# A hybrid attention and SwiGLU layer on one core: every SBUF tile that TensorE reads moved to a multiple of 512 bytes

## The chip, the core and the metric

The kernel runs on one core of a Trainium2 chip. The metric is device time in microseconds (us): three runs of the kernel before gave 1419.07, 1419.39 and 1425.46, median 1419.39. Besides these there is one profiled execution, from which all rows below come.

An SBUF address here is a number of bytes inside a partition. For every tile only its *residue* matters in what follows: its start address modulo 512.

## The reference, cut to what matters

One layer over 256 latent tokens `x` and 256 context tokens `ctx`, all float32, width 2048:

```python
mod = silu_c @ w_ada + b_ada                        # six rows of 2048: shift, scale, gate, twice
h   = rms_norm(x,   g_attn) * (1 + sc_a)  + sh_a
hc  = rms_norm(ctx, g_attn) * (1 + csc_a) + csh_a
q, k, v of four head groups = h @ w_in, hc @ w_in   # neighbourhood, GQA, latent (MLA), differential
x = x + gt_a * (concat(attention outputs) @ w_out)
h = rms_norm(x, g_ffn) * (1 + sc_f) + sh_f
x = x + gt_f * ((silu(h @ ffn_wg) * (h @ ffn_wu)) @ ffn_wd)   # inner width 5632
return rms_norm(x, g_final)
```

The large products with `w_in`, `w_out`, `ffn_wg`, `ffn_wu` and `ffn_wd` are nearly all of the work.

## The kernel before

**Products in three parts.** Each float32 operand is split into a high part of type float32r and a low part (the rest, again float32r). `split` (line 119) makes `whi` from a loaded weight tile `raw` with a copy on ScalarE (ACT, line 127) and `wlo` with a subtraction on VectorE (DVE, line 130). The activations have such pairs too: `h` (hi and lo) for the first layer norm, `o_hi`/`o_lo` for the attention outputs (line 878), `h2_hi`/`h2_lo` for the second norm (line 911), `ah`/`al` for the SwiGLU product (line 1024). `mm3s` (line 145) then issues three matmuls per product, at lines 150, 151 and 153. In most of them the *stationary* operand (loaded into the array, 128 x 128) is a slice of the activations of 128 tokens, and the *moving* operand is a row of 512 weight columns. In the names of the profile the moving operand stands first: `acc<-whi,h_hi` streams `whi` past `h_hi`. Each matmul has its own weight load on PEld, which reads the stationary operand of the next matmul while the present one still streams.

**The order of the work.** The main stream goes through the weights in tiles of 256 x 512 (`stream_w`, one DMA of 512 KB on SyncE's queue each, four `raw` buffers, six `whi` and six `wlo`). From one such tile come 12 matmuls of 512 columns for two token tiles. Side tasks (softmax, transposes, the adaLN columns of `w_ada`) are traced in between by `side.pump`, by times written in the program.

**The stages.** To about 300 us: adaLN, the norm, and the columns of NA and GQA with moving `whi`/`wlo` and stationary `h`. To about 560 us: the other columns and the attention heads. Then the output projection (stationary `o_hi`, `o_lo`); its last third and the first block of SwiGLU keep their weight tiles in the pool `rt` (`keep_w`, line 920: the first tile of each of the two comes from the stream pool, the other seven from `rt`). Then SwiGLU: blocks of gate and up (`gu`, line 986, stationary `h2`) and of down (line 1047, stationary `ah`, `al`). The last 512 columns are done one token tile after the other: the first four weight tiles of token tile 0 are held in a pool `rt2` (line 1067), the others in the stream pool.

**Where tiles lie.** Pools are stacks: those of the left side grow from `const` upwards, those of `side="right"` from the top of SBUF downwards. A tile's address is the sum of the sizes below it, in steps of 32 bytes. So an odd-sized small tile shifts all that lies behind it on its side: `ss2` (line 872) shifts what comes behind it in `res`, `ss3` (line 1010) what comes behind it in `ff`:

```python
small = ctx.enter_context(tc.tile_pool(name="small", bufs=6))     # line 82
ss2 = res.tile([P, 2, 4], F32, name="ss2")                        # line 872
ss3 = ff.tile([P, 2, 5], F32, name="ss3")                         # line 1010
```

Of the kernel before, what the change touches and what calls it, by code (L numbers as in the profile page):

```python
# [10 lines left out]
F32 = mybir.dt.float32  # L11
# [6 lines left out]
P = 128  # L18
# [13 lines left out]
class Side:  # L32
    """Instructions traced in between the weight tiles of the main stream.

    A task is a generator that yields (time it takes of the tensor engine, time its
    results need) in us; its next stage is traced once the main stream has gone on
    for that long. Lanes are worked on independently, `width` tasks of a lane at once.
    """

# [48 lines left out]
def hybrid_dit_kernel(ctx: ExitStack, tc: tile.TileContext, a, out):  # L88
    nc = tc.nc
    pe, act, dve, pool, sp = nc.tensor, nc.scalar, nc.vector, nc.gpsimd, nc.sync  # L90
    side = Side()

    const = ctx.enter_context(tc.tile_pool(name="const", bufs=1))
    small = ctx.enter_context(tc.tile_pool(name="small", bufs=6))
    stream = ctx.enter_context(tc.tile_pool(name="stream", bufs=3))
    dram = ctx.enter_context(tc.tile_pool(name="dram", bufs=1, space=bass.MemoryType.DRAM))
    psA = ctx.enter_context(tc.tile_pool(name="psA", bufs=4, space=PSUM))
    psM = ctx.enter_context(tc.tile_pool(name="psM", bufs=4, space=PSUM))

    po, p_h, p_kv, p_s0 = ExitStack(), ExitStack(), ExitStack(), ExitStack()  # L100
# [4 lines left out]

    # ------------------------------------------------------------ helpers
    def misc():
# [13 lines left out]
    def split(raw, n, keep=None):  # L121
        """hi and lo parts of raw [128, k, n], one pair per k"""
        out_ = []
        pool_, bufs = keep or (stream, WB)
        for k in range(raw.shape[1]):
            hi = pool_.tile([P, n], F32R, name="whi", tag="whi", bufs=bufs)
            act.copy(hi, raw[:, k])  # L127
            newest["act"] = nc.cur_bb.bb.instructions[-1]
            lo = pool_.tile([P, n], F32R, name="wlo", tag="wlo", bufs=bufs)
            dve.tensor_tensor(out=lo, in0=raw[:, k], in1=hi.bitcast(F32), op=ALU.subtract)  # L130
            newest["dve"] = nc.cur_bb.bb.instructions[-1]
            out_.append((hi, lo))
        return out_
# [5 lines left out]
    def after(*ins):  # L139
        """what the block traces on an engine of ins is issued behind them"""  # L140
        st = ExitStack()
        for i in ins:
            st.enter_context(tc.issue_after(i))
        return st

    def mm3s(jobs, w_left=False):
        """l @ r from their parts for each (bank, l, r, start, stop); the products with the
        low part of the weights come after all the others"""
        for dst, l, r, start, stop in jobs:
            pe.matmul(dst, lhsT=l[0], rhs=r[0], start=start, stop=False)  # L150
            pe.matmul(dst, lhsT=l[0 if w_left else 1], rhs=r[1 if w_left else 0], start=False, stop=False)  # L151
        for dst, l, r, start, stop in jobs:
            pe.matmul(dst, lhsT=l[1 if w_left else 0], rhs=r[0 if w_left else 1], start=False, stop=stop)  # L153
# [13 lines left out]

    # ------------------------------------------------------------ tokens and small vectors
    x_t = {}
# [14 lines left out]

    ident = const.tile([P, P], F32, name="ident")
    make_identity(nc, ident)
# [26 lines left out]

    # ------------------------------------------------------------ normalised tokens, features on partitions
    xnT = [None] * 8
# [34 lines left out]
    def ada_pe(pr):  # L250
        """shift and scale of chunks 2 pr, 2 pr + 1 for both streams: column tile j of the
        tensor engine takes chunk j % 2 of the shift (j < 2) or the scale"""
        mv = misc()
        for k2 in range(0, KC, 2):
            raw = sb0.tile([P, 2, 2, 256], F32, name="araw", tag="araw", bufs=4)
            for kk in range(2):
                sp.dma_start(raw[:, kk], ada_two[:, k2 + kk, :, pr * 256:(pr + 1) * 256])
            for kk in range(2):
                kc = k2 + kk
                for j in range(4):  # L260
                    pe.matmul(mv[32 * j:32 * j + 32, :P], lhsT=cs32[:, kc, :], rhs=raw[:, kk, j // 2, tsl(j % 2)], start=(kc == 0), stop=(kc == KC - 1), skip_group_check=True)  # L261
            yield 0.5, 1.3
        mvs = sb0.tile([P, P], F32, name="mvs", bufs=2)
        act.copy(mvs, mv[:, :P])
        yield 0.0, 0.5
        cp = misc()
        pe.transpose(cp[:, :P], mvs, ident)
        cpv = cp[:, :P].rearrange("p (s j t) -> p s j t", s=2, j=2)[:, :, :, 0:2]
        k2 = slice(2 * pr, 2 * pr + 2)

        def col(c):
            return c.unsqueeze(2).to_broadcast([P, 2, 2])

        dve.tensor_tensor(out=scg[:, k2, :], in0=cpv[:, 1], in1=col(colA1[:, 16 + 2 * pr:18 + 2 * pr]), op=ALU.add)
        dve.tensor_tensor(out=scg[:, k2, :], in0=scg[:, k2, :], in1=col(colB[:, k2]), op=ALU.mult)
        dve.tensor_tensor(out=sha[:, k2, :], in0=cpv[:, 0], in1=col(colA[:, k2]), op=ALU.add)
        yield 0.1, 0.0
# [35 lines left out]

    # ------------------------------------------------------------ NA and GQA columns: summed over groups of K chunks on SBUF
    na_qT = kv.tile([P, 4, S], F32, name="qT", bufs=3)
# [5 lines left out]

    # ---- second use of w_ada: gate and FFN columns
    mcol = {s: const.tile([P, KC], F32, name=f"mcol{s}") for s in (2, 3, 4, 5)}
# [31 lines left out]
    parts = [[0], [1], [2, 3], [4, 5], [6, 7]]  # L355
# [7 lines left out]
    def block(c0, prs, first, units):  # L363
        """one block of 512 columns over the K chunks of prs; a unit is (matmul operands, where its bank is added)"""
        accs = [acc() for _ in units]
        for pr in prs:
            w = stream_w(w_in, 2 * pr, c0, 512)
            for i, (form, where) in enumerate(units):
                mm3s([form(accs[i], w, 2 * pr + kk, pr == prs[0] and kk == 0, pr == prs[-1] and kk == 1) for kk in range(2)], c0 == NA_K)
                if pr == prs[-1]:  # L370
                    for dst, src in where(accs[i]):
                        add_up(dst, src, first)
                side.pump(1.3, 2.0)
# [31 lines left out]
    tabs, bias = {}, []  # L405
# [3 lines left out]
    def prepare():  # L409
        """rope tables with the GQA gains in them, the NA bias with its mask, lambda"""  # L410
        xa = sb0.tile([P, 2, 4, S], F32, name="xa", tag="x_t", bufs=2)
# [8 lines left out]
        mask = xb[:, 768:832]  # L420
# [76 lines left out]

    # ------------------------------------------------------------ the four head groups
    p_at = ExitStack()
# [22 lines left out]
    def proj(c0, n, toks, evac, hook=None):  # L522
        """columns c0.. of the input projection for token tiles toks; evac(t, psum) is a task"""
        accs = [acc() for _ in toks]
# [26 lines left out]
    def rope(dst, src, ct, st, nh, hd):  # L551
        """dst = src * ct + swap(src) * st over nh heads of width hd; ct, st [128, hd]"""
        half = hd // 2
# [9 lines left out]
    def soft(score, bias=None):  # L563
        """exp(score - max) of a [128, 512] score tile, and the reciprocal of its sum"""
        if bias is not None:
# [44 lines left out]
    def gate_rows(seg, pool_):  # L610
        """the gate of seg as one row on all partitions, by way of DRAM"""
        ps = misc()
# [17 lines left out]

    # ---- grouped-query attention
    def head_rstd(ps, nh):
# [53 lines left out]

    # ---- multi-head latent attention
    c64, s64 = table("rope_c64", 64), table("rope_s64", 64)
# [109 lines left out]

    # ---- differential attention
    def dk_evac(t, ps):  # L800
# [63 lines left out]

    # ------------------------------------------------------------ output projection and residual
    side.finish(*gate_tasks)
# [4 lines left out]
    gta = gate_rows(2, res)  # L871
    ss2 = res.tile([P, 2, 4], F32, name="ss2")
    p_o3, p_oh = ExitStack(), ExitStack()
# [89 lines left out]

    # ------------------------------------------------------------ SwiGLU
    def gu_jobs(ps, w_, k2, t):
# [43 lines left out]
    gate_f = add_ada(5, 4.0, stream_raw)  # L1009
    ss3 = ff.tile([P, 2, 5], F32, name="ss3")  # L1010
    gfin = ff.tile([P, D], F32, name="gfin")
# [45 lines left out]

    # ------------------------------------------------------------ the last columns one token tile after the other, final norm
    p_h2.close()
# [89 lines left out]
```

## Time and profile before

| | before |
|---|---|
| median of three runs | 1419.39 us |
| span of the profiled execution, first to last instruction | 1415.0 us |
| difference, what lies around the span | 4.4 us |
| PE (matmuls) busy | 1375.5 us, 97% |
| DVE busy | 914.9 us, 65% |
| ACT busy | 618.9 us, 44% |
| HBM traffic | 221 GB/s over the span |
| mean granted TensorE clock | 0.996 of full speed |

The duration that the profile gives for a matmul overlaps with the next one. What a matmul costs in a dense row of matmuls is the distance from its start to the next start; the rows of the timeline give the starts.

### The profile page before, as it was taken

How to read it: one execution, taken by the hardware profiler on the slowest of the kernel's cores; microseconds unless marked ns; L12 is line 12 of the kernel's file. 1: busy time of each engine (PE TensorE's matmuls, PEld its weight loads, DVE VectorE, ACT ScalarE, POOL GpSimd, SP SyncE). 2: the span in 40 equal slices, each digit the busy share in tenths (PEclk: the TensorE clock that was granted, in tenths of full speed). 3: DMA queues.
4: the chain of work that ended last, by engine and by line, in shares of the span. 5: the costliest groups of instructions: out<-in, count | busy, mean ns of one | idle time of the engine just before them, and what ended most of it. 6: DMA issues, size and time to landing. Idle time of an engine off the chain costs nothing.

```text
span 1415.0 us, 19888 instructions
## 1 busy us (share of the span) xinstructions
PE 1375.5 (97%) x7082; PEld 1082.3 (76%) x7082; DVE 914.9 (65%) x1623; ACT 618.9 (44%) x1180; POOL 34.1 (2%) x46
## 2 busy tenths in 40 slices
PE   6999999998999999999999999999999999999997
PEld 4766778766876687777877788888888888888886
DVE  3565679988888728779677854445545565555465
ACT  3522223464333525557444454444444443444443
POOL 1020000100000000000000000000000000000000
PEclk9999999999999999999999999999999999999999
DMA  9998896668879726356888876666666556666653
GB/s 324 322 318 278 282 312 215 205 215 264 270 246 298 230 90 235 124 175 188 290 272 281 293 239 194 185 190 180 191 182 183 182 182 196 183 188 181 185 167 139
DMA packets 183607, 313.78 MB, mean 222 GB/s; under 512 B 14002, under 2 KB 53972, under 8 KB 182356
## 3 DMA queue, kind: packets, MB, share of 16 engines
q1 hardware_dynamic: 179104, 302.03, 66.9%
q0 software_dynamic: 1056, 7.36, 1.3%
q10 hardware_dynamic: 3348, 3.13, 0.7%
q8 instruction: 55, 0.90, 0.3%
q14 instruction: 44, 0.36, 0.1%
HBM read 310.36 MB, written 2.11 MB: 221 GB/s over the span
## 4 chain that ended last, share of the span: by engine, by line
PE 74%; DMA 12%; DVE 8%; ACT 2%; issue 2%; POOL 0%; SPq 0%; ACTq 0%; POOLq 0%; DVEq 0%
PE acc L150 23%; PE acc L151 22%; PE acc L153 22%; DMA raw<-in_w_ada_dram 7%; DVE ada_acc L337 3%; DMA raw<-in_w_in_dram 3%; PE m L261 3%; DVE wlo L130 2%; DMA raw<-in_ffn_wg_dram 1%; ACT whi L127 1%; PE m L830 1%; DMA raw<-in_ffn_wu_dram 1%; DMA rowsB<-in_rows_dram 1%; PE m L232 1%; PE m L541 1%
## 5 line engine op out<-in xcount | busy, mean ns | idle before, releaser
L130 DVE TENSOR_TENSOR wlo<-raw,whi 128x512 fp32r<-128x512 f32 (+1 forms) x764 | 491.2, 682 | 354.0 <-ACT whi L127 345.8
L127 ACT CAST whi<-raw 128x512 fp32r<-128x512 f32 (+1 forms) x764 | 433.0, 614 | 618.6 <-PE acc L151 414.1
L150 PE MATMUL acc<-whi,h_hi 128*128 128x512 f32 x704 | 280.7, 399 | 2.5 <-ACT whi L127 2.5
L151 PE MATMUL acc<-whi,h_lo 128*128 128x512 f32 x704 | 279.1, 396 | 0.0
L153 PE MATMUL acc<-wlo,h_hi 128*128 128x512 f32 x704 | 195.7, 397 | 0.2 <-DVE wlo L130 0.2
L337 DVE SCALAR_TENSOR_TENSOR ada_acc<-raw,cs,ada_acc 128x512 f32<-128x512 f32 x210 | 157.1, 748 | 38.0 <-DMA raw<-in_w_ada_dram 28.7
L150 PE MATMUL acc<-whi,h 128*128 128x512 f32 (+1 forms) x416 | 166.8, 403 | 5.3 <-ACT whi L127 3.4
L150 PEld LDWEIGHTS acc<-whi,h_hi 128*128 128x128 f32 x704 | 132.6, 188 | 36.3 <-ACT whi L127 5.1
L151 PE MATMUL acc<-whi,h 128*128 128x512 f32 (+1 forms) x416 | 157.8, 381 | 0.0
L153 PEld LDWEIGHTS acc<-wlo,h_hi 128*128 128x128 f32 x704 | 132.6, 188 | 32.8 <-DVE wlo L130 0.7
L151 PEld LDWEIGHTS acc<-whi,h_lo 128*128 128x128 f32 x704 | 132.6, 188 | 31.4
L150 PE MATMUL acc<-whi,ah 128*128 128x512 f32 (+1 forms) x364 | 141.3, 390 | 0.0
L151 PE MATMUL acc<-whi,al 128*128 128x512 f32 (+1 forms) x364 | 140.9, 389 | 0.0
L153 PE MATMUL acc<-wlo,h 128*128 128x512 f32 (+1 forms) x416 | 114.4, 379 | 0.2 <-DVE wlo L130 0.2
L150 PEld LDWEIGHTS acc<-whi,h 128*128 128x128 f32 x416 | 78.3, 188 | 30.5 <-issue 11.0
L153 PE MATMUL acc<-wlo,ah 128*128 128x512 f32 (+1 forms) x364 | 98.7, 389 | 0.0
L153 PEld LDWEIGHTS acc<-wlo,h 128*128 128x128 f32 x416 | 76.0, 188 | 15.7 <-DVE wlo L130 1.4
L151 PEld LDWEIGHTS acc<-whi,h 128*128 128x128 f32 x416 | 78.4, 188 | 12.5 <-issue 1.2
L150 PEld LDWEIGHTS acc<-whi,ah 128*128 128x128 f32 x364 | 68.6, 188 | 15.5
L151 PEld LDWEIGHTS acc<-whi,al 128*128 128x128 f32 x364 | 68.6, 188 | 15.4
L153 PEld LDWEIGHTS acc<-wlo,ah 128*128 128x128 f32 x364 | 67.7, 188 | 15.6
L150 PE MATMUL acc<-whi,o_hi 128*128 128x512 f32 x128 | 51.8, 406 | 0.0
(228 smaller groups left out, 1278.6 us busy)
## 6 DMA issues: line engine op xcount, KB each, us to landing
raw<-in_w_ada_dram SPq DMA_DIRECT2D x112, 512.0 KB, 4.6
raw<-in_ffn_wg_dram SPq DMA_DIRECT2D x88, 512.0 KB, 3.8
raw<-in_ffn_wu_dram SPq DMA_DIRECT2D x88, 512.0 KB, 3.9
raw<-in_ffn_wd_dram SPq DMA_DIRECT2D x88, 512.0 KB, 4.6
raw<-in_w_in_dram SPq DMA_DIRECT2D x72, 512.0 KB, 5.0
araw<-in_w_ada_dram SPq DMA_DIRECT2D x128, 256.0 KB, 4.8
raw<-in_w_out_dram SPq DMA_DIRECT2D x32, 512.0 KB, 3.9
araw<-in_w_ada_dram SPq DMA_DIRECT2D x16, 512.0 KB, 5.7
```

The source lines that it names most:

```text
L127: act.copy(hi, raw[:, k])
L130: dve.tensor_tensor(out=lo, in0=raw[:, k], in1=hi.bitcast(F32), op=ALU.subtract)
L150: pe.matmul(dst, lhsT=l[0], rhs=r[0], start=start, stop=False)
L151: pe.matmul(dst, lhsT=l[0 if w_left else 1], rhs=r[1 if w_left else 0], start=False, stop=False)
L153: pe.matmul(dst, lhsT=l[1 if w_left else 0], rhs=r[0 if w_left else 1], start=False, stop=stop)
L232: pe.transpose(ps[:, kk * S + t * P:kk * S + (t + 1) * P], x_t[2 * w + t][:, tsl(2 * pr + kk)], ident)
L261: pe.matmul(mv[32 * j:32 * j + 32, :P], lhsT=cs32[:, kc, :], rhs=raw[:, kk, j // 2, tsl(j % 2)], start=(kc == 0), stop=(kc == KC - 1), ski ...
L337: dve.scalar_tensor_tensor(out=acc_, in0=raw[:, kk, :], scalar=cs[:, 0, kc:kc + 1], in1=acc_, op0=ALU.mult, op1=ALU.add)
L541: pe.transpose(ps[:, tsl(j)], src[:, tsl(j)], ident)
L830: pe.matmul(sc, lhsT=df_qT[hb, h, tsl(t)], rhs=df_kT[h // 2][hb, h % 2, :], start=True, stop=True)
```

## The change

Two pads are added, one on each side, and three small tiles move. `ss2` and `ss3` go into `const`, `ident` into a pool of its own behind a pad of 32 bytes, and a pad of 480 bytes stands at the outer end of the right side.

```diff
     const = ctx.enter_context(tc.tile_pool(name="const", bufs=1))
+    ss2 = const.tile([P, 2, 4], F32, name="ss2")
+    ss3 = const.tile([P, 2, 8], F32, name="ss3")
     small = ctx.enter_context(tc.tile_pool(name="small", bufs=6))
+    pad = ctx.enter_context(tc.tile_pool(name="pad", bufs=1))
+    pad.tile([P, 8], F32, name="left_pad")
+    ident = pad.tile([P, P], F32, name="ident")
     stream = ctx.enter_context(tc.tile_pool(name="stream", bufs=3))
...
+    edge = ctx.enter_context(tc.tile_pool(name="edge", bufs=1, side="right"))
+    edge.tile([P, 120], F32, name="edge_pad")
...
-    ident = const.tile([P, P], F32, name="ident")
...
-    ss2 = res.tile([P, 2, 4], F32, name="ss2")
...
-    ss3 = ff.tile([P, 2, 5], F32, name="ss3")
```

The rest of the diff blanks comments. The built programs have the same instructions in the same order on all five engines. One wait differs: GpSimd's load of `gfin` (used from line 1045 on) no longer waits for four DMA queues, only for DVE, PE and ACT.

The residues (start address modulo 512) as the built programs have them:

| tiles | before | after |
|---|---|---|
| `raw`, `whi`, `wlo` of the stream pool; `h` | 384 | 0 |
| `o_hi`, `o_lo`; `whi`, `wlo` in `rt` | 416 | 0 |
| `h2_hi`, `h2_lo`; `ah`, `al`; `whi`, `wlo` in `rt2` | 480 | 0 |
| all of the right side (`cqT`, `ckvT`, `qT`, `kT`, `v`, `pT`, `p`, `tok`, `x_t`, `araw`, ...) | 480 | 0 |
| `ident` | 256 | 0 |

Slices that TensorE reads from these tiles start at multiples of 512 bytes behind the tile's start (128 float32 columns are 512 bytes), so a slice has its tile's residue. Only the slices of `cs32` (32 columns) do not.

## Rows read from the trace of the kernel before

**Rows 1.** The page, busy time of PE: us, share, instructions.

```profile
PE 1375.5 (97%) x7082; PEld 1082.3 (76%) x7082; DVE 914.9 (65%) x1623; ACT 618.9 (44%) x1180; POOL 34.1 (2%) x46
```

**Rows 2.** Windows: stretch, length, busy us per engine, PEclk, DMA share, GB/s.

```profile
680.00:765.00 85.00, 83.80 (x369) 66.91 (x368) 63.37 (x101) 35.10 (x62) 0.00 (x0) 1.00 0.82 277
1000.00:1100.00 100.00, 100.00 (x437) 80.61 (x436) 49.99 (x78) 44.05 (x78) 0.00 (x0) 1.00 0.62 184
```

**Rows 3.** The chain in order of time: start us, us, what.

```profile
676.67 5.56 DMA raw<-in_w_ada_dram
...
800.55 3.78 DMA raw<-in_ffn_wg_dram
...
1006.34 0.94 PE acc L153 x4
```

**Rows 4.** Timeline of PE near the end: start us, us, line, operands.

```profile
1379.71 1.10 PE L153 MATMUL acc<-wlo,ah 128*128 128x512 f32 x4
...
1388.14 1.10 PE L153 MATMUL acc<-wlo,ah 128*128 128x512 f32 x4
1389.08 0.39 PE L150 MATMUL acc<-whi,ah 128*128 128x512 f32 x1
...
1394.53 0.40 PE L150 MATMUL acc<-whi,ah 128*128 128x512 f32 x1
...
1395.93 0.39 PE L150 MATMUL acc<-whi,ah 128*128 128x512 f32 x1
```

**Rows 5.** Timeline of PE, weights kept in the pool rt.

```profile
635.42 0.39 PE L150 MATMUL acc<-whi,o_hi 128*128 128x512 f32 x1
...
638.14 0.39 PE L150 MATMUL acc<-whi,o_hi 128*128 128x512 f32 x1
...
647.09 0.39 PE L150 MATMUL acc<-whi,h_hi 128*128 128x512 f32 x1
...
649.89 0.39 PE L150 MATMUL acc<-whi,h_hi 128*128 128x512 f32 x1
```

**Rows 6.** Timeline of PE, output projection from the stream pool.

```profile
588.07 1.10 PE L153 MATMUL acc<-wlo,o_hi 128*128 128x512 f32 x4
...
590.87 1.10 PE L153 MATMUL acc<-wlo,o_hi 128*128 128x512 f32 x4
```

**Rows 7.** Timeline of PE, input projection, 512 columns.

```profile
511.72 1.07 PE L153 MATMUL acc<-wlo,h 128*128 128x512 f32 x4
...
514.44 1.07 PE L153 MATMUL acc<-wlo,h 128*128 128x512 f32 x4
```

**Rows 8.** Groups of PE, 800 to 1400 us, by form: count, busy us, mean ns.

```profile
L150 PE MATMUL acc<-whi,h_hi 128*128 128x512 f32 x498 | 198.1, 398 | 0.2 <-ACT whi L127 0.2
L151 PE MATMUL acc<-whi,h_lo 128*128 128x512 f32 x499 | 197.8, 396 | 0.0
L153 PE MATMUL acc<-wlo,h_hi 128*128 128x512 f32 x500 | 137.4, 396 | 0.0
L150 PE MATMUL acc<-whi,ah 128*128 128x512 f32 x340 | 135.0, 397 | 0.0
```

**Rows 9.** Groups of PE on the page, whole span.

```profile
L150 PE MATMUL acc<-whi,h_hi 128*128 128x512 f32 x704 | 280.7, 399 | 2.5 <-ACT whi L127 2.5
L150 PE MATMUL acc<-whi,o_hi 128*128 128x512 f32 x128 | 51.8, 406 | 0.0
```

**Rows 10.** Groups of DVE and ACT that make or use pairs, 800 to 1400 us.

```profile
L130 DVE TENSOR_TENSOR wlo<-raw,whi 128x512 fp32r<-128x512 f32 x425 | 273.8, 688 | 253.7 <-ACT whi L127 250.5 <-PE acc L153 3.0
L127 ACT CAST whi<-raw 128x512 fp32r<-128x512 f32 x424 | 242.0, 618 | 322.7 <-PE acc L151 305.8 <-DMA raw<-in_ffn_wg_dram 7.6 <-DMA raw<-in_ffn_wd_dram 3.3
L1042 DVE TENSOR_TENSOR x<-x,y 128x512 f32<-128x512 f32 x6 | 3.8, 682 | 0.0
```

**Rows 11.** Timeline of PE, input projection, 320 columns.

```profile
364.92 0.75 PE L153 MATMUL acc<-wlo,h 128*128 128x320 f32 x4
...
368.44 0.75 PE L153 MATMUL acc<-wlo,h 128*128 128x320 f32 x4
```

## The prediction

> **What bounds the kernel now.** I read the page's busy times first: PE is busy for 1375.5 of 1415.0 us [rows 1], so TensorE is the first suspect, but such a share does not say whether anything else sets its pace. The windows and the chain of waits do, stage by stage [rows 2, 3]. Between 680 and 765 us DMA has a share of 0.82 and 277 GB/s, PE is idle for 1.2 us, and the chain passes through DMA landings and DVE; its last such piece in the first half of SwiGLU is a landing that starts at 800.55 us. Behind it the chain is PE alone up to the last matmul. In the window from 1000 to 1100 us PE is busy for 100.00 of 100.00 us at the full granted clock (1.00), with DMA at 0.62, DVE at 49.99 us and ACT at 44.05 us. So for the last 600 us the time is the number of matmuls times the distance from one start to the next. The diff changes no instruction. Whether it changes the time hangs on one question: does that distance depend on where the operands lie?
>
> **The trace of before answers it by accident**, since its pools have three residues. I looked for places where the same code runs with other residues, and divided the time between starts by the matmuls between them.
>
> - Near the end, moving `whi`/`wlo` of the stream pool (384), stationary `ah`/`al` (480): from 1379.71 to 1388.14 us stand 36 matmuls of 512 columns, 8.43 / 36 = 0.2342 us each [rows 4].
> - The next 24 are the same loop with the weights held in `rt2`, which lies at 480 as `ah` does: 1389.08 to 1394.53 us, 5.45 / 24 = 0.2271 us. Then the stream pool again: six in 1.40 us, 0.2333 us [rows 4].
> - In `rt`, weights at 416 with `o_hi`/`o_lo` at 416: 12 in 2.72 us, 0.2267 us. A few us later the same pool with `h2` at 480: 12 in 2.80 us, 0.2333 us [rows 5].
> - Output projection, 384 against 416: 12 in 2.80 us, 0.2333 us [rows 6]. Input projection, `whi` and `h` both at 384: 12 in 2.72 us, 0.2267 us [rows 7].
>
> Equal residues (384, 416 or 480 alike) give 0.2267 us, unequal ones 0.2333 to 0.2342 us. So it is not the place of one operand but whether moving and stationary rows start at the same place in a frame of 512 bytes. That fits what happens at a time: PEld reads the next stationary slice while the matmul streams its row, and both read SBUF. It is not the region of SBUF either: `rt` is one pool and shows both values. After the change every pair is equal, at 0.
>
> [...]
>
> **The change part by part.** The durations are those of the profiled execution. Its span of 1415.0 us lies 4.4 us below the median of 1419.39 us; I take the gain from the median and leave the 4.4 us as they are.
>
> *Term A, 800 to 1400 us.* The groups count 498 + 499 + 500 matmuls with `h2` and three groups of 340 with `ah`/`al` (one is shown), 2517 in all [rows 8]. Of these the 24 with `rt2` are equal already, which leaves 2493. Each goes from 0.2342 to 0.2267 us: 2493 x 7.5 ns = 18.7 us. Nothing hides this, since PE is the chain there. What is late next? Twelve matmuls would take 2.72 us; in that time ACT makes two casts of 618 ns, DVE two subtractions of 688 ns [rows 10], and the queue brings 512 KB, that is 524,288 bytes / 2.72 us = 193 GB/s against the 277 GB/s that it delivered between 680 and 765 us [rows 2]. None of them becomes the bound.
>
> *Term B, before 800 us.* Of 3 x 128 matmuls with `o` [rows 9], 84 are equal already (seven of eight kept weight tiles, twelve each): 300 x 6.6 ns = 2.0 us. Of 3 x 704 with `h2`, 1497 lie behind 800 us [rows 8, 9]: 615 x 7.5 ns = 4.6 us. Bounds are 0, if the landings and DVE on the chain keep the pace, and 6.6 us, if PE does. The rows are near the second (PE idle 1.2 of 85 us), the chain near the first; I take half, 3.3 us.
>
> *Term C, the latent projection.* 48 matmuls of 512 columns take `ckvT` at 480 against weights at 384: at most 48 x 7.5 ns = 0.4 us. 95 of 256 columns are unequal too (with `cqT`, and in the last columns): at most 95 x 7.5 ns = 0.7 us. Between 0 and 1.1 us I take 0.2 us, since these stand among attention heads that wait for ACT.
>
> *At nothing.* The first 560 us have pairs at 384 alike, as in rows 7, and their rate stays. DVE does not mind residues: the subtraction with all tiles at 384 takes 688 ns, the addition on `x2` (384) and `y` (480) takes 682 ns [rows 10]. The load of `gfin` may start earlier; it is used only from the last group of SwiGLU on, hundreds of us later. `ss2`, `ss3` and `ident` are the same reads and writes elsewhere.
>
> The sum is 18.7 + 3.3 + 0.2 = 22.2 us, and 1419.4 - 22.2 = 1397.2 us. I forecast 1397 us.
>
> **The rivals.**
>
> 1. *No change.* Something that goes with the residues makes the difference, such as the pool or the stage, and 1419 us stay. For it speaks only that nobody has seen residue 0. Against it: two places where the value turns within one loop [rows 4] or one pool [rows 5], and three pairs that agree at 0.2267 us. [...]
>
> 2. *Half the gain.* With PE faster, the landings and the `wlo` of the stretch up to 800 us stay late (term B is 0), and in term A waits grow for half of what is saved: 1419.4 - 9.4 = 1410 us. The rates in term A speak against it. Chance 0.05.
>
> 3. *More than the gain.* An equal pair may still pay for crossing a border of 512 bytes, which no tile of before avoids: every row starts at 384, 416, 480 or, for `ident`, 256. The size of this: 24 matmuls of 320 columns take 3.52 us, 0.1467 us each [rows 11], so 192 columns cost 0.0800 us, 0.417 ns a column. Then 512 columns cost 0.2133 us, and 13.4 ns of the 226.7 ns do not depend on the columns. If all of these went, 2517 x 13.4 ns = 33.7 us more would come in term A's stretch alone, and the time would be near 1363 us. That three residues agree at 0.2267 us speaks against a dependence on the place as such, and a remainder that is the same for 320 and 512 columns is as well the price of changing the weights. Chance 0.05. [...]
>
> 4. *Slower.* At residue 0 both reads start at the border of a frame, and if that is where they collide, the equal pairs take the slow distance or more. With all pairs at 0.2342 us, the 1356 of 512 columns that are equal now (1248 of the input projection by the built program, 84 with `rt`, 24 with `rt2`) lose 1356 x 7.5 ns = 10.2 us, and the time is 1430 us. It decides from a distance of 0.2321 us on, where the gain of the 3456 unequal matmuls (48 + 300 + 2112 + 996 with `ah`) equals the loss of the 1356. For it: zero is untried. Against it: nothing sets 0 apart from 384, if only the difference of the two counts. Chance 0.04.
>
> **How the numbers follow.** My forecast has 0.80, with a range of its own from 1392 to 1404 us: term B from 0 to 6.6 us, the 0.8 ns or so by which the distances are uncertain (2 us over 2493), and a few us for scatter (the three runs lie within 6.4 us). The range given, 1388 to 1409 us, holds most of this and reaches towards rival 2; rivals 1, 3 and 4 lie outside, 0.15 together. Half a per cent is about what a measurement of this kernel can tell from no change, so faster means under 1412.3 us and slower over 1426.5 us. Forecast and rivals 2 and 3 are faster: 0.90. Rival 1 is the same: 0.06. Rival 4 is slower: 0.04.
>
> **What would show it.** In the profile after, twelve matmuls of 512 columns with `h2` or `ah` stand 2.72 us apart in place of 2.80 to 2.82 us, and those with `h` stay at 2.72 us. The last matmul comes some 22 us earlier, of which about 19 us were gained behind 800 us. Between 680 and 800 us DVE's and ACT's idle time on landings grows. The steps are wrong if `h2` and `ah` still show 2.81 us (rival 1), if PE gains idle time behind 800 us (rival 2), if the distance for 512 columns falls clearly under 0.226 us (rival 3), or if the input projection rises over 2.72 us (rival 4).

## The result and the profile after

The changed kernel took 1397.7 us (median of 4 runs, 1393.33 to 1401.37) against 1419.72 us (1419.07 to 1425.46), a ratio of 0.9843 (95% interval in brackets, here and below: [0.982, 0.9865]); 1397 us was forecast. The profiled execution spans 1396.4 us, before 1415.0 us.

The busy times and the shares of the chain on the page of the changed kernel. PE is busy for 19.2 us less than in [rows 1], about what the span lost.

```profile
PE 1356.3 (97%) x7082; PEld 1080.1 (77%) x7082; DVE 913.2 (65%) x1623; ACT 619.1 (44%) x1180; POOL 34.6 (2%) x46
...
PE 77%; DMA 11%; DVE 6%; ACT 2%; issue 2%; POOL 0%; ACTq 0%; SPq 0%; POOLq 0%; DVEq 0%
```

The windows of [rows 2] again, in the changed kernel: stretch and its length, busy us (x instructions) of PE, PEld, DVE, ACT and POOL, granted clock, DMA share, GB/s.

```profile
680.00:765.00 85.00, 81.33 (x360) 64.32 (x360) 63.27 (x100) 34.53 (x62) 0.00 (x0) 1.00 0.81 270
1000.00:1100.00 100.00, 100.00 (x451) 82.95 (x450) 51.42 (x80) 45.48 (x82) 0.00 (x0) 1.00 0.65 189
```

The two stages part here. Behind 1000 us PE is still never idle, at the same granted clock (1.00), and 451 matmuls fit where 437 did. Between 680 and 765 us PE is idle for 3.7 us instead of 1.2 us, and 360 matmuls fit where 369 did.

The timeline of PE in the changed kernel: start, us, line, operands. Line 160 was 150 and line 163 was 153. The first pair of starts answers to [rows 4], the others to [rows 5] and [rows 7].

```profile
1361.56 1.07 PE L163 MATMUL acc<-wlo,ah 128*128 128x512 f32 x4
...
1369.72 1.07 PE L163 MATMUL acc<-wlo,ah 128*128 128x512 f32 x4
1370.62 0.39 PE L160 MATMUL acc<-whi,ah 128*128 128x512 f32 x1
...
1376.06 0.39 PE L160 MATMUL acc<-whi,ah 128*128 128x512 f32 x1
...
644.70 0.39 PE L160 MATMUL acc<-whi,h_hi 128*128 128x512 f32 x1
...
647.42 0.39 PE L160 MATMUL acc<-whi,h_hi 128*128 128x512 f32 x1
...
510.52 1.07 PE L163 MATMUL acc<-wlo,h 128*128 128x512 f32 x4
...
513.24 1.07 PE L163 MATMUL acc<-wlo,h 128*128 128x512 f32 x4
```

The 36 matmuls with `ah` take 8.16 us (0.2267 each) in place of 8.43; the 24 that were equal before still take 5.44 us; twelve with `h2` from `rt` take 2.72 us in place of 2.80, and so do twelve of the output projection (585.94 to 588.66 us); the input projection keeps its 2.72 us.

To see where the lead arises I took one kind of instruction that every version issues in the same place: the transposes of the SwiGLU product. There are eleven groups of them; the first, the fourth and the last serve as marks and are called the first, second and third transposes below. Their rows before, then after (start, us):

```profile
698.99 1.04 PE L1003 MATMUL m<-ident,sg 128*128 128x128 f32 x8
...
842.33 0.93 PE L1003 MATMUL m<-ident,sg 128*128 128x128 f32 x7
...
1343.24 0.93 PE L1003 MATMUL m<-ident,sg 128*128 128x128 f32 x7
```

```profile
695.48 0.71 PE L1011 MATMUL m<-ident,sg 128*128 128x128 f32 x5
...
841.11 1.03 PE L1011 MATMUL m<-ident,sg 128*128 128x128 f32 x8
...
1326.21 1.03 PE L1011 MATMUL m<-ident,sg 128*128 128x128 f32 x8
```

The lead is 3.5 us at the first, 1.2 us at the second, 17.0 us at the third and 18.6 us at the end. So the last stretch gives 15.8 + 1.6 us; the stretch between the first two became 2.3 us longer (143.34 to 145.63), although its matmuls are shorter. The waits view of that stretch, 699 to 842 us, names the reason: engine, line, what it waited for, us in total, times, longest. Before, then after:

```profile
PEld acc L150 <- ACT whi L127: 5.1, 8, 1.5
...
PE acc L150 <- ACT whi L127: 2.5, 4, 1.1
```

```profile
PEld acc L160 <- ACT whi L137: 9.5, 18, 1.8
...
PE acc L160 <- ACT whi L137: 4.0, 6, 1.4
...
PEld acc L163 <- DVE wlo L140: 3.3, 6, 1.7
...
PE acc L163 <- DVE wlo L140: 1.2, 1, 1.2
```

TensorE's waits for the parts of the weights grew from 7.6 to 18.0 us (the loads' waits partly run beside matmuls, so the sum is not idle time of PE: PE's own waits grew from 2.5 to 5.2 us).

### The profile page after: what moved, and what is told of

Its sections match the earlier page's. It is cut to its first block, busy times and chain, and to the rows that moved or that the text cites. A ratio compares the mean times of both kernels' runs of the same rounds, so it can differ in the third digit from the quotient of the medians.

```text
span 1396.4 us, 19886 instructions
## 1 busy us (share of the span) xinstructions
PE 1356.3 (97%) x7082; PEld 1080.1 (77%) x7082; DVE 913.2 (65%) x1623; ACT 619.1 (44%) x1180; POOL 34.6 (2%) x46
## 4 chain that ended last, share of the span: by engine, by line
PE 77%; DMA 11%; DVE 6%; ACT 2%; issue 2%; POOL 0%; ACTq 0%; SPq 0%; POOLq 0%; DVEq 0%
PE acc L160 24%; PE acc L161 23%; PE acc L163 23%; DMA raw<-in_w_ada_dram 5%; PE m L270 2%; DVE wlo L140 2%; DVE ada_acc L346 2%; DMA raw<-in_w_in_dram 2%; DMA araw<-in_w_ada_dram 1%; DMA raw<-in_ffn_wg_dram 1%; DMA raw<-in_ffn_wu_dram 1%; ACT whi L137 1%; PE m L601 1%; PE m L550 1%; PE m L839 1%
## 5 line engine op out<-in xcount | busy, mean ns | idle before, releaser
L160 PE MATMUL acc<-whi,h_hi 128*128 128x512 f32 x704 | 276.6, 393 | 4.2 <-ACT whi L137 4.0
L161 PE MATMUL acc<-whi,h_lo 128*128 128x512 f32 x704 | 274.3, 390 | 0.0
L163 PE MATMUL acc<-wlo,h_hi 128*128 128x512 f32 x704 | 191.8, 391 | 1.6 <-DVE wlo L140 1.4
L161 PEld LDWEIGHTS acc<-whi,h 128*128 128x128 f32 x416 | 78.7, 189 | 12.9 <-issue 1.4
L160 PE MATMUL acc<-whi,o_hi 128*128 128x512 f32 x128 | 51.4, 402 | 0.0
```

## The experiments

Theory: a matmul of 512 columns takes 7 ns longer where its moving row and stationary slice start at different places of a frame; equality counts, not zero. Rivals: zero itself, or the border of 512 bytes, counts; or the pool or stage does. A second question is why the stretch from 699 to 842 us gave nothing.

**The distance by itself.** A kernel of nothing but groups of 24 matmuls; in a name such as `m0s32q` the moving row starts 0 bytes and the stationary slice 32 bytes into tiles that lie at residue 0; `n384` is the number of columns.

```diff
+    def group(name, m, s, n=512, count=24, step=0):
+        ps = ps_.tile([P, 512], F32, name=name, tag="acc", bufs=4)
+        m, s = m // 4, s // 4
+        for i in range(count):
+            pe.matmul(ps[:, :n], lhsT=st[:, s:s + P], rhs=mv[:, m:m + n], start=i == 0, stop=i == count - 1)
...
+    for s in list(range(0, 512, 32)) + [512, 1024, 1536, 2048, 4096]:
+        group(f"m0s{s}q", 0, s)
```

> A kernel that leaves out the whole computation: groups of 24 dense float32r matmuls whose moving row starts m bytes and whose stationary slice starts s bytes into two tiles at residue 0 (group names m..s..q); nothing else runs beside them. Theory 1 (equal residues): m0s0 and all groups with m = s (32 to 480) stand 0.2267 us apart, m0s512 to m0s4096 too; groups with m unlike s 0.231 to 0.238 us; which differences count is open, and the groups m0s32 to m0s480 and m0s4 to m0s28 say it. Rival A (an operand's own border of 512 bytes): groups m0s* and m*s0 differ from each other, and m = s is not better than the unequal groups with the same m. Rival B (no read contention at all, the stage made the difference): all groups of 512 columns alike, about 0.227 us. In the groups with turns the slow distance falls on every second matmul.

The timeline of that kernel, one row for a group of 24; the distance is the difference of two consecutive starts, divided by 24.

```profile
26.59 5.61 PE L52 MATMUL m0s0q<-mv,st 128*128 128x512 f32 x24
32.03 5.75 PE L52 MATMUL m0s32q<-mv,st 128*128 128x512 f32 x24
37.62 5.76 PE L52 MATMUL m0s64q<-mv,st 128*128 128x512 f32 x24
...
65.54 5.76 PE L52 MATMUL m0s224q<-mv,st 128*128 128x512 f32 x24
71.14 5.61 PE L52 MATMUL m0s256q<-mv,st 128*128 128x512 f32 x24
76.59 5.75 PE L52 MATMUL m0s288q<-mv,st 128*128 128x512 f32 x24
...
383.95 4.33 PE L52 MATMUL n384s0q<-mv,st 128*128 128x384 f32 x24
388.11 4.32 PE L52 MATMUL n384s32q<-mv,st 128*128 128x384 f32 x24
392.27 4.33 PE L52 MATMUL n384s96q<-mv,st 128*128 128x384 f32 x24
```

A difference of 0 gives 5.44 / 24 = 0.2267 us, of 32 bytes 5.59 / 24 = 0.2329 us: the effect stands without any pool, stage or other engine. Equal pairs at any of the residues tried give 0.2267 to 0.2283 us, unequal ones with the stationary slice at 0 (`m32s0q` and so on) mostly the same 0.233 to 0.234 us as those with the moving row at 0, so neither operand has a border of its own. But the frame is 256 bytes, not 512: a difference of 256 gives 5.45 / 24 = 0.2271 us. And it costs only with many columns: with 384, both differences of starts are 4.16 us, 0.1733 us a matmul, and with 128 (110 to 112 ns), 256 (118 to 122 ns) and 320 (146.7 ns) no difference stood out either. Two parts were missed. Where two places take turns, 0 and 96, I had every second matmul down as slow; they do not alternate, and the mean is 230 ns. And four groups with a difference (stationary less moving) of -64 bytes modulo 256 (`m0s192q`, `m0s448q`, `m64s0q`, `m320s0q`) gave an intermediate 0.2292 to 0.2296 us. Differences of 4 to 28 bytes, on which the expectation left things open, gave 0.2300 to 0.2350 us without order.

**One side only.** The left side at 0, the right side (`h2`) left at 480:

```diff
-    edge = ctx.enter_context(tc.tile_pool(name="edge", bufs=1, side="right"))
-    edge.tile([P, 120], F32, name="edge_pad")
```

> The change without the pad of the right side: stream pool, rt, o and ah at 0, h2 and the whole right side at 480. Theory 1: pairs with h2 (2112 matmuls, 1497 of them behind 800 us) keep 0.2342 us, those with ah and o fall to 0.2267 us; against the changed kernel the time is 11 us longer, about 1408 us. Rival A with the moving row as the operand that must be aligned: the same time as the changed kernel, about 1397 us, since every large moving row lies at 0. Rival B: 1419 us.

It took 1405.85 us (1403.85 to 1407.87), 0.9905 [0.9879, 0.993] of before. Its timeline of PE, twelve matmuls with `h2` and twelve with `ah`:

```profile
1001.49 1.09 PE L161 MATMUL acc<-wlo,h_hi 128*128 128x512 f32 x4
...
1004.29 1.09 PE L161 MATMUL acc<-wlo,h_hi 128*128 128x512 f32 x4
...
1151.10 1.07 PE L161 MATMUL acc<-wlo,ah 128*128 128x512 f32 x4
...
1153.82 1.07 PE L161 MATMUL acc<-wlo,ah 128*128 128x512 f32 x4
```

2.80 us and 2.72 us: within one kernel the price goes to just those matmuls whose pair is unequal. Against the changed kernel in the same session (below) it costs 8.4 us, where I had 11. I had taken 0.2342 us for these pairs, but 0 against 480 takes 0.2333 us; and the stretch up to 842 us gave nothing here either. Between the second and the third transposes stand 1344 matmuls with `h2`, and this stretch takes 493.9 us in place of 485.1, 8.8 us more, 6.5 ns a matmul.

**Equal, but not at zero.** Everything at 32 bytes past the border:

```diff
-    pad.tile([P, 8], F32, name="left_pad")
+    pad.tile([P, 16], F32, name="left_pad")
...
-    edge.tile([P, 120], F32, name="edge_pad")
+    edge.tile([P, 112], F32, name="edge_pad")
```

> The change with both pads altered by 32 bytes so that every tile that TensorE reads, on both sides, lies at residue 32. Theory 1 (only equality counts): the time of the changed kernel, about 1397 us, and 2.72 us for twelve matmuls. Rival A (the multiple of 512 counts): back to 1415 to 1420 us, and 2.80 us.

1396.58 us (1394.31 to 1399.42), 0.9834 [0.9804, 0.9863], the whole gain, and twelve matmuls with `h2` take 2.72 us (1000.82 to 1003.54 us). Multiples of 512 bytes are not needed. Beside it stood the changed kernel as it is:

> The changed kernel once more, for comparison on the same chip: 1397 us by every theory.

1397.44 us (1395.49 to 1399.46), 0.9845 [0.982, 0.987].

**Narrower weights.** If the loading of the weights took turns with the moving row, a slice of 32 columns, with a quarter of the bytes, should lose less. The second sweep also had column counts between 384 and 512.

```diff
+            pe.matmul(ps[:w, :n], lhsT=st[:, s:s + w], rhs=mv[:, m:m + n], start=i == 0, stop=i == count - 1)
...
+    for w in (32, 64, 96, 128):
+        for s in (0, 32, 128):
+            wide(f"w{w}s{s}q", 0, s, w)
```

> Again a kernel that leaves out the whole computation, groups of 24 dense float32r matmuls. Groups w..s..q: stationary slices of 32 to 128 columns; n..s..q: 384 to 512 moving columns; s is the difference in bytes. Theory 1 in detail (the read of the next weights takes turns with the row's stream): for differences of 32 and 128 bytes the extra of 6.7 ns shrinks with the width of the stationary slice, about half at 64 columns, and it comes in gradually between 384 columns (no extra) and 512. Rival (the extra comes from the start of the row itself, not from the weight load): the extra is the same 6.7 ns at all widths. Pairs with m - s of 256 (m32s288, m96s352, m160s416, m416s160): 0.2267 us; the others 0.233 us.

Its timeline, slices of 32 columns at a difference of 0, 32 and 128 bytes:

```profile
27.38 5.72 PE L78 MATMUL w32s0q<-mv,st 128*32 128x512 f32 x24
32.94 5.87 PE L78 MATMUL w32s32q<-mv,st 128*32 128x512 f32 x24
38.65 5.70 PE L78 MATMUL w32s128q<-mv,st 128*32 128x512 f32 x24
44.19 5.68 PE L78 MATMUL w64s0q<-mv,st 128*64 128x512 f32 x24
```

5.56 / 24 = 0.2317 us when equal, 5.71 / 24 = 0.2379 us when 32 apart, and 5.54 / 24 = 0.2308 us when 128 apart: the narrow slice is slower even when equal, and its extra is 6 ns at one difference and nothing at the other. All widths, from starts divided by 24 in the same way, in ns:

| stationary columns | equal | 32 apart | 128 apart |
|---|---|---|---|
| 32 | 231.7 | 237.9 | 230.8 |
| 64 | 229.6 | 231.7 | 229.6 |
| 96 | 230.4 | 228.8 | 231.7 |
| 128 | 227.5 | 233.3 | 231.7 |

The extra neither shrinks evenly with the width, as the theory had it, nor stays at 6.7 ns, as the rival had it. So whether anything takes turns inside TensorE is not shown. By moving columns, equal against 32 apart: 180.0 and 183.3 ns at 400, 187.9 and 190.0 at 416, 196.3 and 199.6 at 432, 202.9 and 204.6 at 448, 210.0 and 210.8 at 464, 217.1 and 219.6 at 480, 223.3 and 226.3 at 496, 228.8 and 232.9 at 512. At 384 there is no extra again (174.6 and 173.3). It does not grow evenly either, and at 432 columns 128 bytes apart cost nothing (195.0 ns). Pairs 256 apart at other places gave 226.7 to 228.3 ns, 384 against 480 gave 233.8 ns and 384 against 416 gave 233.3 ns, as in [rows 4, 6]. Moving 160 against stationary 96, which is again a difference of -64, gave 233.7 ns: the intermediate value of the first sweep does not go with the difference alone.

**Why nothing came through between 699 and 842 us.** First theory: too many bytes stand in that stretch. The last adaLN segment, streamed there, was spread over more time:

```diff
-    gate_f = add_ada(5, 4.0, stream_raw)
+    gate_f = add_ada(5, 9.0, stream_raw)
...
-        if gi == 0:
+        if gi == 1:
             side.finish(*gate_f)
```

> The changed kernel with the last adaLN columns (segment 5) traced at intervals of 9.0 us in place of 4.0, and finished one SwiGLU group later. Theory (DMA landings between 690 and 820 us swallow the gain of term B): with fewer bytes in that stretch PE's waits there go, and the time falls by 3 to 6 us, to about 1392 us. Rival (term B was lost elsewhere, or the loads only collide later): 1397 us or more.

> The kernel before with the same spreading of segment 5. Theory: it gains less than the changed kernel does, 0 to 3 us (1416 to 1419 us), since PE at 0.2342 us a matmul waits less; the difference to the changed kernel with the spreading is then 24 us rather than 21. Rival: both gain alike, or none.

> The changed kernel for comparison on the same chip: 1397 us.

On the changed kernel: 1399.49 us (1395.59 to 1407.25), 0.9878 [0.9853, 0.9904]; on the kernel before: 1418.06 us, 0.9998 [0.9983, 1.0013]; the changed kernel beside them: 1397.47 us (1396.56 to 1401.67), 0.9865 [0.9844, 0.9886]. No gain, a miss; the two versions with the spreading stand 18.6 us apart where I had 24. The spread version was 9 us ahead of the changed kernel beside it at the second transposes and lost it by about 1000 us. Two of its waits from 842 to 1000 us:

```profile
DVE ada_acc L346 <- DMA raw<-in_w_ada_dram: 46.7, 12, 4.9
...
PEld acc L163 <- DVE wlo L140: 10.9, 18, 1.7
```

The queue was less full there (DMA share 0.70 and 229 GB/s between 900 and 1000 us, against 0.81 and 270 GB/s above), yet DVE waited for twelve adaLN tiles, 3.9 us each. In its timeline the `wlo` that TensorE needs come right behind such a wait (in brackets, us):

```profile
904.20 0.75 DVE L346 SCALAR_TENSOR_TENSOR ada_acc<-raw,cs,ada_acc 128x512 f32<-128x512 f32 x1 [4.06 <-DMA raw<-in_w_ada_dram]
904.87 1.29 DVE L140 TENSOR_TENSOR wlo<-raw,whi 128x512 fp32r<-128x512 f32 x2
```

New theory: what costs is the wait of DVE for a tile asked for just before, not the bytes. So the tile is asked for one visit of the adaLN task earlier, into three buffers of its own:

```diff
+            due[0] = max(due[0] + gap, side.now - 4 * gap)
+            if lead:
+                yield 0.0, max(0.0, due[0] - side.now)
...
-            due[0] = max(due[0] + gap, side.now - 4 * gap)
-            yield 0.0, max(0.0, due[0] - side.now)
+            if not lead:
+                yield 0.0, max(0.0, due[0] - side.now)
...
+    def gate_raw(src, shape):
+        raw = ff.tile(shape, F32, name="graw", bufs=3)
+        sp.dma_start(raw, src)
+        return raw
...
-    gate_f = add_ada(5, 4.0, stream_raw)
+    gate_f = add_ada(5, 4.0, gate_raw, lead=True)
```

> The changed kernel in which the tiles of w_ada for segment 5 have three buffers of their own (not the stream pool's raw) and are loaded one step (4 us) before DVE uses them. Theory (between 690 and 820 us PE waits because DVE stands behind an adaLN tile that was asked for only just before, and its loads take buffers from the weights): PE's waits of that stretch go, the gain of term B comes through, and the time falls by 4 to 8 us to about 1391 us. Rival (the bytes themselves are the limit there, 280 GB/s): 1397 us, the same as the changed kernel.

> The same edit on the kernel before. Theory: with 0.2342 us a matmul there was less waiting to take away, so it gains 0 to 4 us (1414 to 1418 us) and the difference between the two residues with this edit is 22 to 24 us. Rival (the bytes are the limit): 1418 us, and the difference stays about 20 us.

> The changed kernel for comparison on the same chip: 1397 us.

On the changed kernel: 1389.15 us (1387.10 to 1393.10), 0.9785 [0.9761, 0.9808], faster than the kernel before and than the changed kernel. On the kernel before: 1412.27 us (1411.19 to 1415.93), 0.9953 [0.9936, 0.9971]; I had expected 1414 us or more. The changed kernel beside them: 1395.42 us (1394.56 to 1399.25), 0.9832 [0.9806, 0.9857]. The window from 700 to 820 us, in the kernel before and in the changed kernel, then in both (in the same order) with the early request:

```profile
700.00:820.00 120.00, 117.54 (x515) 92.98 (x514) 89.18 (x142) 52.92 (x95) 0.00 (x0) 1.00 0.84 282
```

```profile
700.00:820.00 120.00, 114.36 (x501) 89.29 (x500) 89.32 (x142) 53.30 (x96) 0.00 (x0) 1.00 0.83 278
```

```profile
700.00:820.00 120.00, 120.00 (x531) 96.86 (x531) 92.70 (x148) 54.52 (x98) 0.00 (x0) 1.00 0.83 286
```

```profile
700.00:820.00 120.00, 120.00 (x546) 99.53 (x545) 92.62 (x149) 55.63 (x98) 0.00 (x0) 1.00 0.84 288
```

PE is idle for 2.5 and 5.6 us without the edit and not at all with it, where more bytes move: the bytes were not the limit. Whether it was DVE's wait, as the new theory has it, is another matter. Waits from 699 to 842 us in the changed kernel, then with the edit:

```profile
ACT whi L137 <- DMA raw<-in_ffn_wu_dram: 25.7, 13, 3.8
...
ACT whi L137 <- DMA raw<-in_ffn_wg_dram: 21.8, 10, 3.9
...
DVE ada_acc L346 <- DMA raw<-in_w_ada_dram: 14.0, 11, 4.3
```

```profile
SPq L125 <- DVE ada_acc L346: 17.9, 24, 2.4
```

```profile
DVE ada_acc L349 <- DMA graw<-in_w_ada_dram: 12.0, 9, 2.6
...
ACT whi L137 <- DMA raw<-in_ffn_wg_dram: 5.1, 3, 1.9
```

DVE still waits 12.0 us for adaLN landings where it waited 14.0. What goes is the wait of SyncE, which issues the loads, for DVE to give back a `raw` buffer that holds an adaLN tile (17.9 us; with the edit no adaLN tile of that segment lies in one), ACT's wait for the weights' landings (47.5 to 5.1 us), and with it all of TensorE's 18.0 us. That points to the buffers more than to the early request; the two were changed together, and which of them does it is open.

With PE's waits gone in both, the residues are worth in this stretch what the matmuls say. The transposes in the version made from the changed kernel, then in the one made from the kernel before:

```profile
694.81 1.04 PE L1014 MATMUL m<-ident,sg 128*128 128x128 f32 x8
...
830.15 1.03 PE L1014 MATMUL m<-ident,sg 128*128 128x128 f32 x8
```

```profile
698.49 1.04 PE L1006 MATMUL m<-ident,sg 128*128 128x128 f32 x8
...
837.89 1.03 PE L1006 MATMUL m<-ident,sg 128*128 128x128 f32 x8
```

135.34 against 139.40 us: 4.1 us for the 576 unequal matmuls in between, 7.0 ns each, where the pair without the edit shows a loss of 2.3 us. The medians do not show this: those of the two versions with the edit stand 23.1 us apart, and those of the same session without it 23.8 us.

## Why the prediction came out

- **The step on the residues held.** Every unequal pair timed above fell to 0.2267 us, and the equal ones stayed. That the cause is the pair, not something that goes with it, was argued from three accidents in the trace before; the sweep and the two pads now show it. Too coarse was the frame: it is 256 bytes (0.2271 us at a difference of 256), and at the widths tried up to 384 columns no extra stood out, so none shows for the 95 matmuls of 256 columns in term C (the sweep gives 118 to 122 ns, without order). The reason that the prediction leaned towards, that the load of the next weights and the row's stream get in each other's way, is not shown: the extra does not follow the width of the load (6.2, 2.1, -1.6 and 5.8 ns at 32, 64, 96 and 128 columns, 32 bytes apart).
- **Term A** was 18.7 us behind 800 us. Behind the second transposes, at 842 us, 15.8 + 1.6 = 17.4 us are measured, and the 2316 unequal matmuls that stand there give 17.4 us at 7.5 ns; the 42 us ahead of them belong to the stretch that waits. Only its rate at 480 depended on the partner: 0.2342 us against 384 [rows 4], 0.2333 us against 0 (twelve in 2.80 us).
- **Term B** was taken as 3.3 us between 0 and 6.6. In the profiled pair 1.2 us stand at 842 us, and as much, 1.2 us, is there at the first matmul with `o` (531.1 against 529.9 us), ahead of every pair that the term counts. So by this pair it came to nothing: 2.3 us were won up to 699 us and 2.3 us lost again up to 842 us, which is the bound "if the landings and DVE on the chain keep the pace". The other profiles of the changed kernel say the same. From the first matmul with `o` to the second transposes the kernel before takes 311.3 us, and four profiled runs of the changed kernel take 310.0 to 312.4 us; from there to the third transposes all four take 485.1 us in place of 500.9. With the early request, where waits no longer take it, the same stretch from `o` on takes 307.2 us in the version made from the kernel before and 300.9 us in the other: 6.2 us, where the rates of the prediction would give 7.9 (300 x 6.6 ns and 792 x 7.5 ns). This rests on one profile of each.
- **The total was met partly by luck.** The medians differ by 22.0 us (19.2 to 25.6) and the sum was 22.2, but the profiles account for the 17.4 us of term A and for 1.2 us that come ahead of every pair that the terms count. The remaining 3.4 us are not placed: the first matmul with `o` starts between 527.1 and 529.9 us in the four profiles, and in four sessions the medians of the two kernels stand 20.2 to 23.8 us apart. Term B at 3.3 us is thus not borne out, though its bounds hold; term C, 0.2 us, is too small to see, and no run measures it by itself.
- **The signs.** Named and seen: 2.72 us per twelve, the input projection unchanged, PE without idle time behind 842 us. Named and hardly seen: DVE's waits for adaLN landings between 699 and 842 us grew from 12.9 to 14.0 us. Named and not seen: ACT's waits for the weights' landings fell there, from 51.4 to 47.5 us. What grew were TensorE's waits for `whi` and `wlo`, from 7.6 to 18.0 us, which I had only at the bound. The last matmul came 18.5 us earlier in the profiled pair, not 22.
- **The rivals.** No change fell with the result. Half the gain was right that term B is 0 in the profiled pair and wrong on the waits in term A, of which there are none behind 842 us. More than the gain fell with the result: at residue 0 the equal pairs keep 0.2267 us, so the remainder of 13.4 ns did not go; in the sweep 384 columns have it too (173.3 ns, less 160 ns by 0.417 ns a column). Slower fell with the input projection, whose pairs went from 384 to 0 and kept 2.72 us.

## What to carry to other kernels

Where TensorE is never idle, read the distance from start to start of the same matmul at several places of the trace: if it takes two values, look for what differs in the operands, down to their addresses. In float32r matmuls of 512 columns try moving rows and stationary slices that agree modulo 256 bytes (226.7 to 228.8 ns in place of 232 to 234 ns in the two sweeps); here pads of 32 and 480 bytes, each ahead of a pool, and three moved tiles did it. A faster engine gave nothing in the stretch where it waited for what others make (143.34 us became 145.63): look there for a side task that holds buffers of the main stream, and try buffers of its own for it and an earlier request.

## What the runs showed of the hardware

- In the two sweeps, matmuls in float32r of 128 x 128 weights and 512 columns start 226.7 to 228.8 ns apart if both operands start at the same byte modulo 256. At other differences in steps of 32 bytes they start 232 to 234 ns apart, but for four groups 64 bytes apart (229 ns); at 4 to 28 bytes, 230 to 235 ns. With 128, 256, 320 and 384 columns no order by places shows (110 to 112, 118 to 122, 146.7, 173 to 176 ns); from 400 to 496 columns a difference of 32 bytes cost 0.8 to 3.3 ns.
- Narrower stationary slices were not faster: equal pairs take 231.7 ns with 32 columns of weights, 226.7 to 228.8 ns with 128. Why, and why the effect shows at 400 moving columns (180.0 and 183.3 ns) and not at 384 (174.6 and 173.3 ns), stays open.
- An early request with three buffers of its own for the side task's tiles was worth 6 to 7 us in this kernel at a DMA share of 0.83 to 0.84. The queue delivered more with it in the changed kernel: 288 in place of 278 GB/s between 700 and 820 us.
